# The product p @ W_ple moved from the attention stage to the opening, and x loaded a second time, turned, in a hybrid decoder layer

## The chip, the cores and the metric

The kernel runs on one core of one Trainium2 chip. The metric is the time of one execution on the device in microseconds (us). A core has five instruction streams that matter here: TensorE (PE, with its weight loads PEld), VectorE (DVE), ScalarE (ACT), GpSimd (POOL) and SyncE (SP), whose queue issues every DMA of this kernel, in order.

## The reference, cut to what matters

One decoder layer over 1024 tokens of width 1024, in float32:

```
h = RMSNorm(x)                                   # x: 1024 x 1024
proj = h @ W_in                                  # all projections, indexer keys i_k among them
o_A = gated DeltaNet(...) * SiLU(z_A)            # 4 heads
o_B = top-256 sparse attention(...) * SiLU(z_B)  # 8 heads
x = x + concat(o_A, o_B) @ W_out
gate = sigmoid(RMSNorm(x) @ W_gate + b_gate)
x = x + (p @ W_ple) * gate                       # p: 1024 x 256, W_ple: 256 x 1024
```

p @ W_ple depends on nothing else in the layer; it is needed only in the last line.

## The kernel before

Activations are held turned, features on the 128 partitions and tokens along the row, so that a projection is a chain of matmuls with a weight tile held in the array and 512 tokens streamed. For precision each float32 operand is split into a high part (ScalarE, a copy rounded to the matmul's type) and a low part (the rest, on VectorE or GpSimd), and `mm3` (line 778) takes three matmuls, hi·hi, hi·lo and lo·hi, for each product.

The program is recorded first and then ordered: the class `Plan` (from line 276) takes every instruction as an operation with a price (`price`, 339), list-schedules them (`forward` 466, `backward` 521), scores some orders by playing them (`play` 422) and issues the best (`issue` 556). Every instruction issued there has line 576 in the profile, so the rows are told apart by tile names. `keep_in_program_order` ties an operation to the one recorded before it on its engine.

The stages, in order:

- **The opening** (`start`, 795). `x_dma` (752) loads x in eight blocks of 128 tokens (tile `xt`, 512 KB each, five buffers), the norm's gain (`gcol`), `w_small` in two parts (`raws`; the columns for K, V and the small projections) and the weights of the indexer's keys (`raww`). `spread_gain` (807) turns the gain into a row tile by 8 transposes; 10 and 24 transposes of the identity around it keep TensorE running. For each block j: `front` (820) takes the sum of squares on ScalarE (`sq`), the reciprocal root on GpSimd (`rs`, two instructions) and x·r·gain on VectorE (`xn`); `turn` (831) makes 8 transposes on TensorE into two PSUM tiles (`xT`); `back` (841) copies them as `hThi` (ScalarE) and `hTlo` (VectorE); `small` (924) is 24 matmuls of 272 columns (`sm`) with the split `w_small` (`his`, `los`), evicted to `sm` and `kv` by ScalarE. Then `ik` (849): 48 matmuls of 512 columns in all, `Pik`.
- **Projections, indexer, DeltaNet** (60 to 540 us): a stream of weight jobs (class `Stream`) with chains of the other work woven in. Weights come as `raww`, split into `hiw` (ScalarE) and `low` (GpSimd).
- **Attention** (from 538 us): scores `S`, softmax on VectorE, ScalarE and GpSimd (`P`), transposes `pt`, products `pv`. The last z projections (`Pbz`) and then the jobs of the string `tail` in `jobs` (1560) fill TensorE beside it: "L" is a job of p @ W_ple, "M" loads the mixer's output, "A" to "D" are the output projection (`oA` to `oD`), "G" and "H" the gate (`g`).
- **p @ W_ple before**: `tail_open` (1842) calls `load_p` (1871), which loads p turned and splits it (`praw`, `pTh`, `pTl`). Eight jobs `ple_job` (1882), one for each quarter of W_ple and half of the tokens, make 12 matmuls of 512 columns each (`ple`), two evictions (`plt`) and two DMAs of 256 KB to memory (`pled`). The gate job (1963) loads them back (`pld`).

## Time and profile before

| | us |
|---|---|
| three runs | 863.83, 865.32, 2914.96 |
| their median | 865.32 |
| the profiled execution, its own time | 864.6 |
| its span, first to last instruction | 862.9 |
| TensorE busy in the span | 836.3 |

The run of 2914.96 us stands apart by a factor of three and is not used. The span is the part of the execution that the trace covers; the profiled execution's own time is 1.7 us more. A busy engine is one with an instruction in flight; TensorE's matmuls overlap, so a row's mean duration is longer than the distance from one matmul to the next.

### The profile page before, as it was taken

The numbers are of one execution on the slowest core, as the hardware profiler recorded it, in microseconds if no ns is written. First come the engines' busy times: TensorE is split into PE (matmuls) and PEld (weight loads), VectorE is DVE, ScalarE is ACT, GpSimd is POOL, SyncE is SP. The second block draws the span as 40 slices with busy tenths as digits, with TensorE's granted clock in tenths as the row PEclk, the third lists the DMA queues.
The fourth block names the chain that finished last, engine by engine and source line by source line (L and its number), as shares of the span: only waits on it lengthen the run. The fifth ranks groups of instructions, "written<-read, shape, count | busy, mean of one in ns | idle before, by whom it ended". The sixth has DMA issues, their size and how long they took to land.

```text
span 862.9 us, 15480 instructions
## 1 busy us (share of the span) xinstructions
PE 836.3 (97%) x5231; PEld 704.6 (82%) x5231; DVE 599.6 (69%) x1394; ACT 581.1 (67%) x1289; POOL 478.6 (55%) x651
## 2 busy tenths in 40 slices
PE   7999999999999999989999999899999999999996
PEld 6887888988778888878878888688888888787885
DVE  5535555567899878898887675978767687646344
ACT  5536465545868988889988843998876577655432
POOL 1162221312765766485775744588775587658841
PEclk9999999999999999999999999899999999999999
DMA  7123111132223222223123225885535321346453
GB/s 274 51 86 99 51 60 36 47 84 66 68 66 99 72 71 60 59 100 91 39 71 99 74 91 181 253 269 181 161 112 172 133 63 50 101 132 220 140 182 105
DMA packets 79455, 94.23 MB, mean 109 GB/s; under 512 B 24176, under 2 KB 40592, under 8 KB 79248
## 3 DMA queue, kind: packets, MB, share of 16 engines
q1 hardware_dynamic: 79376, 93.25, 34.2%
q8 instruction: 41, 0.67, 0.4%
q14 instruction: 38, 0.31, 0.1%
HBM read 67.77 MB, written 25.45 MB: 108 GB/s over the span
## 4 chain that ended last, share of the span: by engine, by line
PE 86%; DVE 4%; DMA 3%; ACT 3%; SPq 1%; issue 1%; POOL 1%; DVEq 0%; ACTq 0%; POOLq 0%
PE g L576 10%; PE Piq L576 8%; PE Pav L576 5%; PE Paz L576 5%; PE lg L576 5%; PE Paq L576 5%; PE Pbq L576 4%; PE Pbz L576 4%; PE pv L576 4%; PE S L576 4%; PE pt L576 4%; PE Pak L576 3%; PE ple L576 3%; PE sm L576 2%; PE po L576 1%; PE xT L576 1%
## 5 line engine op out<-in xcount | busy, mean ns | idle before, releaser
L576 POOL TENSOR_TENSOR low<-raww,hiw 128x512 fp32r<-128x512 f32 x138 | 186.8, 1355 | 170.7 <-ACT hiw L576 108.8
L576 ACT ACTIVATE hiw<-raww 128x512 fp32r<-128x512 f32 x138 | 86.4, 631 | 80.0 <-PE g L576 16.6
L576 ACT ACTIVATE junka<-score,nt 128x1024 bf16<-128x1024 int16 (+1 forms) x96 | 110.3, 1149 | 1.3
L576 DVE TENSOR_SCALAR_CACHE_REDUCE junk<-score,cand 128x384 bf16<-128x384 f32 (+2 forms) x96 | 70.8, 738 | 0.9
L576 POOL TENSOR_SCALAR P<-P,rsum 128x128 f32<-128x128 f32 (+7 forms) x64 | 50.2, 790 | 27.9 <-DVE rsum L576 21.4
L576 ACT ACTIVATE relu<-lg 128x384 f32<-128x384 f32 (+3 forms) x80 | 40.4, 526 | 34.7 <-PE lg L576 32.9
L576 ACT ACTIVATE P<-P,nm,rq 128x128 f32<-128x128 f32 (+7 forms) x64 | 55.2, 864 | 9.9 <-DVE nm L576 9.2
L576 POOL TENSOR_SCALAR nt<-acca,upa 128x1 f32<-128x1 f32 x96 | 34.9, 364 | 46.0 <-ACT junka L576 43.3
L576 DVE SCALAR_TENSOR_TENSOR score<-relu,sm,score 128x384 f32<-128x384 f32 (+5 forms) x42 | 45.7, 1097 | 20.6 <-ACT relu L576 20.1
L576 DVE TENSOR_TENSOR pl<-pt,ph 128x512 fp32r<-128x512 f32 x72 | 48.4, 687 | 13.9 <-ACT ph L576 12.4
L576 ACT ACTIVATE ph<-pt 128x512 fp32r<-128x512 f32 x72 | 42.0, 596 | 22.6 <-PE pt L576 21.8
L576 PE MATMUL S<-kst,qT 128*128 128x384 f32 (+4 forms) x192 | 55.0, 365 | 1.5 <-DVE mx L576 1.5
L576 PE MATMUL pt<-ident,P 128*128 128x128 f32 x288 | 51.7, 278 | 1.2 <-POOL P L576 0.6
L576 PEld LDWEIGHTS pt<-ident,P 128*128 128x128 f32 x288 | 38.1, 143 | 12.8 <-DVE pl L576 1.4
L576 PEld LDWEIGHTS S<-kst,qT 128*128 128x128 f32 x192 | 35.0, 195 | 8.2 <-DVE mx L576 2.5
L576 PE MATMUL Piq<-hThi,low 128*128 128x256 f32 (+1 forms) x128 | 40.7, 344 | 0.0
L576 PE MATMUL Piq<-hThi,hiw 128*128 128x256 f32 (+1 forms) x128 | 40.1, 343 | 0.0
L576 PE MATMUL Piq<-hTlo,hiw 128*128 128x256 f32 (+1 forms) x128 | 38.9, 339 | 0.0
L576 DVE TENSOR_TENSOR gth<-g,rb 128x512 f32<-128x512 f32 x16 | 11.1, 692 | 37.6 <-PE g L576 30.7
L576 DVE CUSTOM_DVE_ANT_0 P<-S,score 128x384 f32<-128x384 f32 (+3 forms) x48 | 28.6, 598 | 11.8 <-PE S L576 9.1
L576 PE MATMUL pv<-ph,vst 128*128 128x512 f32 x72 | 29.9, 416 | 0.0
L576 PE MATMUL pv<-pl,vst 128*128 128x512 f32 x72 | 29.8, 414 | 0.0
(623 smaller groups left out, 2825.6 us busy)
## 6 DMA issues: line engine op xcount, KB each, us to landing
raww<-in_w_ct_dram SPq DMA_DIRECT2D x66, 256.0 KB
raww<-in_w_out_dram SPq DMA_DIRECT2D x32, 256.0 KB
raww<-in_w_gate_dram SPq DMA_DIRECT2D x32, 256.0 KB
xt<-in_x_dram SPq DMA_DIRECT2D x8, 512.0 KB
pled<-plt SPq DMA_DIRECT2D x16, 256.0 KB
pld<-pled SPq DMA_DIRECT2D x16, 256.0 KB
out_dram<-gth SPq DMA_DIRECT2D x16, 256.0 KB
scr<-gcd SPq DMA_DIRECT2D x8, 256.0 KB
```

The costliest lines, as they stand in the source:

```text
L576: r = getattr(getattr(self.nc, o.eng), fn)(*[real(x) for x in args], **{k: real(v) for k, v in kw.items()})
```

## The change

- x is loaded a second time as `xc`, turned by the host's layout (`lay_out`), 512 KB a block in four buffers. The 64 transposes of x and the 8 of the gain go, and so do `xn` and `gain`. In their place `turn` makes one transpose that spreads r over the partitions (`rp`), and VectorE scales xc into PSUM: four instructions of 128 columns by gain and r, and one of 512 by r alone, for which GpSimd has multiplied the second half of xc by the gain.
- p @ W_ple becomes the opening's first work: its first chunk of p and two parts of W_ple lead SP's queue (p's first chunk in two halves), `ple_out(0, 0)` and `ple_out(1, 0)` come before x's first block, and six more stand one beside each of the blocks 1 to 6. p's chunks share the buffers of `xt`; `phi` and `plo` are p's parts. The evictions and the DMAs to `pled` come with them. The "L" jobs leave the tail.
- 30 transposes of the identity stand ahead in one piece (`warm`), and most ties to program order in the opening are dropped.
- The planner's prices change: a DMA occupies SP's queue for 400 and not 120, the backward pass counts a DMA's bytes, and an order's score is that of the play without jitter plus the mean of two with half the jitter.

```diff
-TL, TG = 3, 6
+TG, PLT = 6, 3
-WARM, WARM2 = 10, 24
+WARM = 30
-JITTER = (1, 2, 3)
-
-
+JITTER, UNEVEN = (1, 2), 524288
...
-            op.occ, op.bytes = 120, int(np.prod(o.ix.shape)) * SIZE[o.dt]
+            op.occ, op.bytes = 400, int(np.prod(o.ix.shape)) * SIZE[o.dt]
...
-                t = sum(self.play(o, seed) for seed in JITTER)
+                t = self.score(o)
                 if t < self.best:
                     self.best, order = t, o
         self.issue(order)
+
+    def score(self, order):
+        return self.play(order, 0) + sum(self.play(order, seed) for seed in JITTER) / len(JITTER)
...
-                occ *= 1 + (o.i * 40503 + seed * 30011) % 65536 / 262144
+                occ *= 1 + (o.i * 40503 + seed * 30011) % 65536 / UNEVEN
...
-            free[e] = s + o.occ
+            free[e] = s + max(o.occ, o.bytes / 280)
...
-        self.xt = [self.xpool.tile([128, D], F32, name="xt") for j in range(8)]
-        self.gain = self.xpool.tile([128, D], F32, name="gain", bufs=1)
-        load = lambda j: self.nc.sync.dma_start(self.xt[j], self.a["x"][j * 128:(j + 1) * 128, :])
+        self.xt, self.xc = [], []
+
+        keep = self.tc.keep_in_program_order
+
+        def load(j):
+            self.xt.append(self.xpool.tile([128, D], F32, name="xt"))
+            self.xc.append(self.xpool.tile([128, 8, 128], F32, name="xc", bufs=4))
+            keep(self.nc.sync.dma_start(self.xt[j], self.a["x"][j * 128:(j + 1) * 128, :]))
+            keep(self.nc.sync.dma_start(self.xc[j], self.a["xc"][j]))
...
+        self.gcol = self.xpool.tile([128, 8], F32, name="gcol", bufs=1)
+        self.praw, self.wpl = [], []
+
+        def load_p(n):
+            self.praw.append(self.xpool.tile([128, 2, 512], F32, name="praw", tag="xt"))
+            if n:
+                keep(self.nc.sync.dma_start(self.praw[n], self.a["pT"][n]))
+                return
+            keep(self.nc.sync.dma_start(self.praw[n][:, 0], self.a["pT"][n][:, 0]))
+            load_w(0)
+            keep(self.nc.sync.dma_start(self.praw[n][:, 1], self.a["pT"][n][:, 1]))
+
+        def load_w(e):
+            self.wpl.append(self.wp.tile([128, 4, 128], F32, name="raww", bufs=2))
+            keep(self.nc.sync.dma_start(self.wpl[e], self.a["w_ple"][e]))
+        load_p(0)
+        keep(self.nc.sync.dma_start(self.gcol, self.a["gains"][:, 16:24]))
+        load(0)
+        load_w(1)
+        for g in range(2):
+            keep(self.nc.sync.dma_start(self.wsm[g], self.a["w_small"][:, 4 * g:4 * g + 4]))
+        load(1)
+        load_p(1)
+        for j in range(2, 4):
+            load(j)
+        keep = lambda x: x
+        for e in range(2, 4):
+            load_w(e)
...
-            def spread_gain():
-                ps = [pp.tile([128, 4, 128], F32, name="xT") for _ in range(3)]
...
+            def warm(n):
+                ps = pp.tile([128, 4, 128], F32, name="xT", bufs=4)
+                for k in range(n):
+                    self.tc.keep_in_program_order(nc.tensor.transpose(ps[:, k % 4], self.ident, self.ident))
...
-                n = p.tile([128, D], F32, name="xn", bufs=2)
-                keep(nc.vector.scalar_tensor_tensor(n, x, r, self.gain, op0=OP.mult, op1=OP.mult))
-                return n
-
-            def turn(n):
-                out = []
-                for g in range(2):
-                    ps = pp.tile([128, 4, 128], F32, name="xT")
-                    for k in range(4):
-                        o = (4 * g + k) * 128
-                        keep(nc.tensor.transpose(ps[:, k], n[:, o:o + 128], self.ident))
-                    out.append(ps)
+                nc.gpsimd.tensor_tensor(xc[:, 4:8], xc[:, 4:8],
+                                        self.gcol[:, 4:8, None].to_broadcast([128, 4, 128]), op=OP.mult)
+                return r
+
+            def turn(j, r):
+                xc = self.xc[j]
+                rp = pp.tile([128, 128], F32, name="rp", bufs=1)
+                nc.tensor.transpose(rp, r.to_broadcast([128, 128]), self.ident)
+                out = [pp.tile([128, 4, 128], F32, name="xT", bufs=4) for g in range(2)]
+                for k in range(4):
+                    nc.vector.scalar_tensor_tensor(out[0][:, k], xc[:, k], self.gcol[:, k:k + 1], rp,
+                                                        op0=OP.mult, op1=OP.mult)
+                nc.vector.tensor_tensor(out[1], xc[:, 4:8], rp[:, None, :].to_broadcast([128, 4, 128]), op=OP.mult)
                 return out
...
+            def ple(e):
+                if e < 2:
+                    hi = self.plp.tile([128, 2, 512], F32R, name="phi", bufs=2)
+                    lo = self.plp.tile([128, 2, 512], F32R, name="plo", bufs=2)
+                    pt.append((hi, lo))
+                    if e:
+                        nc.scalar.activation(hi, self.praw[e], AF.Copy)
+                        nc.gpsimd.tensor_tensor(lo, self.praw[e], hi.bitcast(F32), op=OP.subtract)
+                    else:
+                        nc.scalar.activation(hi[:, 0], self.praw[e][:, 0], AF.Copy)
+                        nc.vector.tensor_tensor(lo[:, 0], self.praw[e][:, 0], hi[:, 0].bitcast(F32), op=OP.subtract)
+                whi = self.wp.tile([128, 4, 128], F32R, name="hiw", bufs=4)
+                wlo = self.wp.tile([128, 4, 128], F32R, name="low", bufs=4)
+                if e:
+                    nc.scalar.activation(whi, self.wpl[e], AF.Copy)
+                if not e:
+                    nc.scalar.activation(whi, self.wpl[e], AF.Copy)
+                    nc.scalar.activation(hi[:, 1], self.praw[e][:, 1], AF.Copy)
+                (nc.gpsimd if e else nc.vector).tensor_tensor(wlo, self.wpl[e], whi.bitcast(F32), op=OP.subtract)
+                wp.append((whi, wlo))
+                if not e:
+                    nc.vector.tensor_tensor(lo[:, 1], self.praw[e][:, 1], hi[:, 1].bitcast(F32), op=OP.subtract)
+
+            def ple_out(e, n):
+                (ph, pl), (whi, wlo) = pt[n], wp[e]
+                for j in range(2):
+                    ps = self.mm_ps(f"ple{e}_{n}")
+                    for k in range(2):
+                        self.mm3(ps, whi[:, 2 * j + k], wlo[:, 2 * j + k], ph[:, k], pl[:, k], k == 0, k == 1)
+                    t = self.plp.tile([128, 512], F32, name="plt", bufs=PLT)
+                    nc.scalar.activation(t, ps, AF.Copy, scale=0.5)
+                    nc.sync.dma_start(self.pled[n, 2 * e + j], t)
+
+            pt, wp = [], []
+            self.pled = self.tc.dram_tile([2, 8, 128, 512], F32, name="pled")
...
+            warm(WARM)
+            ple(0)
+            ple_out(0, 0)
+            ple(1)
+            ple_out(1, 0)
+            r = front(0)
+            ps, sm = turn(0, r), ()
+            later = {1: ((0, 1),), 2: ((1, 1),), 3: ((2, 0),), 4: ((2, 1),), 5: ((3, 0),), 6: ((3, 1),)}
             for j in range(9):
-                if j < 7:
-                    n = front(j + 1)
+                for e, n in later.get(j, ()):
+                    if e > 1 and n == 0:
+                        ple(e)
+                    ple_out(e, n)
+                if j == 0:
+                    self.small_split(0)
                 if j < 8:
                     back(j, ps)
+                if j < 7:
+                    r = front(j + 1)
                 if j == 0:
                     self.small_split(1)
                 for _ in sm:
                     pass
-                if j < 7:
-                    ps = turn(n)
                 if j < 8:
-                    if j == 6:
+                    if j == 5:
                         whi, wlo = self.split_w4("ik", self.wik)
                     sm = self.small(j)
                     next(sm)
+                if j < 7:
+                    ps = turn(j + 1, r)
+                if j == 7:
+                    ik(0)
             self.stream.prep(2)
-            ik(0)
             ik(1)
             self.k_norm()
         self.xpool_cm.__exit__(None, None, None)
+        self.plcm.close()
...
-        tail = "L" * TL + "M"
+        tail = "M"
         for d in range(8):
-            tail += "A" + "L" * ((8 - TL) * (d + 1) // 8 - (8 - TL) * d // 8)
+            tail += "A"
         tail += "M" + "C" * 8 + "B" * 8 + "G" * TG + "D" * 8 + "G" * (8 - TG) + "H" * 8
         for c in tail:
             i = cnt[c] = cnt.get(c, -1) + 1
-            if c == "L":
-                self.ple_job(st, i % 4, i // 4)
-            elif c == "M":
+            if c == "M":
...
-        self.pled = self.tc.dram_tile([2, 8, 128, 512], F32, name="pled")
-        self.load_p()
...
-    def ple_job(self, st, e, n):
-        nc = self.nc
-
-        def body(w):
-            (hi, lo), = w
-            ph, pl = self.pT[n]
...
+    o["xc"] = np.ascontiguousarray(g["x"][0].reshape(8, 128, 8, 128).transpose(0, 3, 2, 1))
...
-    o["pT"] = np.ascontiguousarray(g["p"][0, 0].T)
+    o["pT"] = np.ascontiguousarray(g["p"][0, 0].T.reshape(2, 128, 2, 512).transpose(2, 1, 0, 3))
```

TensorE's order at the start of the program, before (names: `sm_134` is the first small block):

```order
L576 MATMUL xT<-ident 128x128 x10
L576 MATMUL xT<-ident,gcol 128x128 x8
L576 MATMUL xT<-ident 128x128 x24
L576 MATMUL xT<-ident,xn 128x128 x16
L576 MATMUL sm_134<-his,hThi 128x272
L576 MATMUL sm_134<-los,hThi 128x272
L576 MATMUL sm_134<-his,hTlo 128x272
```

And with the change (`ple_0_126` and `ple_0_135` are the two halves of the first product):

```order
L581 MATMUL xT<-ident 128x128 x30
L581 MATMUL ple_0_126<-phi,hiw 128x512
L581 MATMUL ple_0_126<-plo,hiw 128x512
L581 MATMUL ple_0_135<-phi,hiw 128x512
L581 MATMUL ple_0_135<-plo,hiw 128x512
L581 MATMUL ple_0_126<-phi,low 128x512
L581 MATMUL ple_0_126<-phi,hiw 128x512
L581 MATMUL ple_0_135<-phi,low 128x512
L581 MATMUL ple_0_135<-phi,hiw 128x512
L581 MATMUL ple_0_126<-plo,hiw 128x512
```

The first product stands where the gain's transposes were. Behind the rows shown come the first `rp`, the 12 matmuls of the second product and then, with the last one among them, the first small block.

ScalarE's order at the start, before:

```order
L576 ACT_TABLE_LOAD
L576 ACTIVATE sq,ss<-xt 128x1024
L576 ACTIVATE his<-raws 128x1088
L576 ACTIVATE sq,ss<-xt 128x1024
L576 ACTIVATE hThi<-xT 128x4x128 x2
L576 ACTIVATE his<-raws 128x1088
L576 ACTIVATE sq,ss<-xt 128x1024
L576 ACTIVATE hThi<-xT 128x4x128 x2
L576 ACTIVATE sm<-sm_134 128x16
L576 ACTIVATE kv<-sm_134 128x256
```

And with the change, from its fifth instruction on (ahead stand the table load and the splits `phi`, `hiw`, `phi`; `ple_0_142` is the second product, `sm_275` the first small block):

```order
L581 ACTIVATE sq,ss<-xt 128x1024
L581 ACTIVATE plt<-ple_0_126 128x512
L581 ACTIVATE plt<-ple_0_135 128x512
L581 ACTIVATE hiw<-raww 128x512
L581 ACTIVATE his<-raws 128x1088
L581 ACTIVATE hThi<-xT 128x4x128 x2
L581 ACTIVATE his<-raws 128x1088
L581 ACTIVATE plt<-ple_0_142 128x512
L581 ACTIVATE sq,ss<-xt 128x1024
L581 ACTIVATE kv<-sm_275 128x256
L581 ACTIVATE sm<-sm_275 128x16
L581 ACTIVATE phi<-praw 128x1024
```

Two evictions and a split of W_ple now stand between the first `sq` and the two `his`, and p's second chunk, `phi` with 1024 columns, stands between the first small block's evictions and the next `hThi`.

TensorE's order at the attention's first blocks, before, where the first job of the tail begins:

```order
L576 MATMUL S_0_6699<-kst,qT 128x384 x2
L576 MATMUL S_1_6705<-kst,qT 128x384 x2
L576 MATMUL pv_1_6708<-ph,vst 128x512
L576 MATMUL pv_1_6708<-pl,vst 128x512
L576 MATMUL S_2_6726<-kst,qT 128x384 x2
L576 MATMUL pt_1_6732<-ident,P_4_6610 128x128
L576 MATMUL pt_1_6732<-ident,P_5_6618 128x128
L576 MATMUL pt_1_6740<-ident,P_4_6610 128x128
L576 MATMUL pt_1_6740<-ident,P_5_6618 128x128
L576 MATMUL S_3_6746<-kst,qT 128x384 x2
L576 MATMUL ple_0_6490<-pTh,hiw 128x512
```

And with the change, where the first job of the tail begins:

```order
L581 MATMUL pt_0_7003<-ident,P_2_6861 128x128
L581 MATMUL pt_0_7003<-ident,P_3_6872 128x128
L581 MATMUL pv_1_7022<-ph,vst 128x512
L581 MATMUL pv_1_7022<-pl,vst 128x512
L581 MATMUL pv_1_7022<-ph,vst 128x512
L581 MATMUL pv_1_7022<-pl,vst 128x512
L581 MATMUL S_0_7027<-kst,qT 128x512 x2
L581 MATMUL S_1_7032<-kst,qT 128x512 x2
L581 MATMUL S_2_7056<-kst,qT 128x512 x2
L581 MATMUL S_3_7069<-kst,qT 128x512 x2
L581 MATMUL oA__6869<-m0Ah,hiw 128x512
```

In both a stretch of `S`, `pt` and `pv` without other matmuls ends where the tail's first job starts, a product before and an `oA` now. It stood at scores of 384 columns, and now reaches those of 512. Behind the attention's first S stand 25 matmuls `Pbz` before and 57 now.

## Rows read from the trace of the kernel before

**Rows 1.** The page: its first line and the busy line of TensorE (busy us, share of the span, instructions).

```profile
span 862.9 us, 15480 instructions
PE 836.3 (97%) x5231; PEld 704.6 (82%) x5231; DVE 599.6 (69%) x1394; ACT 581.1 (67%) x1289; POOL 478.6 (55%) x651
```

**Rows 2.** The list of waits, TensorE alone, over the whole span: who waited, for whom, us in total, times, longest.

```profile
PE xT L576 <- DMA gcol<-in_gains_dram: 3.2, 1, 3.2
...
PE xT L576 <- DVE xn L576: 2.3, 2, 1.8
...
PE ple L576 <- ACT pTh L576: 1.0, 1, 1.0
```

**Rows 3.** Windows: the start up to the first transpose of x. The columns are the stretch, its length, then busy us and instructions of TensorE, its weight loads, VectorE, ScalarE and GpSimd, the granted clock of TensorE, the DMA share and GB/s.

```profile
0.00:13.39 13.39, 8.28 (x42) 7.88 (x43) 5.48 (x13) 4.69 (x6) 2.44 (x13) 1.00 0.78 289
```

**Rows 4.** The timeline of the opening, TensorE and ScalarE: start us, us, engine, line, operation, output and inputs, count, and in brackets the idle time before it and what ended it.

```profile
1.90 2.40 PE L576 MATMUL xT<-ident 128*128 128x128 f32 x10 [1.90 <-DVE ident L576]
...
4.68 1.06 ACT L576 ACTIVATE sq<-xt 128x1024 bf16<-128x1024 f32 x1 [2.61 <-DMA xt<-in_x_dram]
...
6.01 1.11 ACT L576 ACTIVATE his<-raws 128x1088 fp32r<-128x1088 f32 x1 [0.18 <-DMA raws<-in_w_small_dram]
...
7.38 1.06 ACT L576 ACTIVATE sq<-xt 128x1024 bf16<-128x1024 f32 x1 [0.25 <-DMA xt<-in_x_dram]
...
7.51 1.97 PE L576 MATMUL xT<-ident,gcol 128*128 128x128 f32 x8 [3.21 <-DMA gcol<-in_gains_dram]
...
9.27 4.29 PE L576 MATMUL xT<-ident 128*128 128x128 f32 x24
...
13.39 1.91 PE L576 MATMUL xT<-ident,xn 128*128 128x128 f32 x16
...
18.84 0.29 PE L576 MATMUL sm<-his,hTlo 128*128 128x272 f32 x1
```

**Rows 5.** Two windows of the opening, for the transfers: the stretch, its length, the granted clock, the DMA share and GB/s.

```profile
6.00:8.00 2.00, 1.00 1.04 411
22.00:26.00 4.00, 1.00 0.70 229
```

**Rows 6.** Groups by line and shape, 0 to 62 us: engine, operation, output and inputs, shapes, count, then busy us, mean ns of one, and the idle time before them. The last two rows are from the views of the tiles S and xT: their numbers are ns min/median/max and the first and last start in us.

```profile
L576 DVE TENSOR_TENSOR hTlo<-xT,hThi 128x512 fp32r<-128x512 f32 x16 | 10.3, 683 | 1.8 <-ACT hThi L576 1.8
...
L576 ACT ACTIVATE hThi<-xT 128x512 fp32r<-128x512 f32 x16 | 8.7, 601 | 6.5 <-PE xT L576 6.5
L576 ACT ACTIVATE sq<-xt 128x1024 bf16<-128x1024 f32 x8 | 8.5, 1059 | 2.9 <-DMA xt<-in_x_dram 2.9
...
L576 POOL TENSOR_TENSOR low<-raww,hiw 128x512 fp32r<-128x512 f32 x5 | 6.7, 1350 | 5.3 <-ACT hiw L576 5.3
...
L576 POOL TENSOR_TENSOR rs<-rs,mhalf 128x1 f32<-128x1 f32 x8 | 4.4, 553 | 0.7
L576 ACT ACTIVATE hiw<-raww 128x512 fp32r<-128x512 f32 x6 | 3.7, 633 | 1.9 <-DMA raww<-in_w_ct_dram 1.7
L576 ACT ACTIVATE kv<-sm 128x256 f32<-128x256 f32 x8 | 3.0, 379 | 0.0
...
L576 DVE TENSOR_TENSOR los<-raws,his 128x1088 fp32r<-128x1088 f32 x2 | 2.6, 1288 | 0.2 <-ACT his L576 0.2
...
L576 ACT ACTIVATE his<-raws 128x1088 fp32r<-128x1088 f32 x2 | 2.2, 1114 | 0.2 <-DMA raws<-in_w_small_dram 0.2
...
L576 DVE SCALAR_TENSOR_TENSOR S<-S,egl,rec0c x6: 333/344/349, 265.5 to 297.0; 128x128 f32<-128x128 f32 x6
...
L576 PE MATMUL xT<-ident,xn x64: 271/272/303, 13.4 to 42.1; 128*128 128x128 f32 x64
```

**Rows 7.** The chain of work that ended last, in order of time, 0 to 60 us and 500 to 600 us: start us, us, what.

```profile
30.45 3.03 PE sm L576 x24
33.48 0.87 PE xT L576 x8
...
37.39 1.06 PE xT L576 x8
...
53.51 2.09 PE Pik L576 x9
...
562.75 2.28 PE ple L576 x10
```

**Rows 8.** The tile ple, the sum of p @ W_ple, and its eviction to plt: ns min/median/max, first and last start in us.

```profile
L576 PE MATMUL ple<-pTh,hiw x32: 389/397/497, 559.9 to 633.1; 128*128 128x512 f32 x32
...
L576 ACT ACTIVATE plt<-ple x16: 579/598/609, 565.1 to 637.4; 128x512 f32<-128x512 f32 x16
```

**Rows 9.** Windows over the first half of the attention, columns as in rows 3.

```profile
540.00:560.00 20.00, 16.88 (x82) 13.40 (x80) 18.67 (x82) 18.36 (x51) 11.57 (x20) 0.83 0.83 247
560.00:640.00 80.00, 80.00 (x414) 66.27 (x414) 62.25 (x183) 68.82 (x143) 61.33 (x59) 1.00 0.60 191
640.00:660.00 20.00, 20.00 (x105) 16.93 (x104) 13.84 (x39) 14.40 (x28) 14.62 (x14) 1.00 0.46 148
```

**Rows 10.** Windows at the attention's first blocks, columns as in rows 3.

```profile
550.00:552.00 2.00, 1.38 (x7) 1.07 (x7) 1.94 (x10) 1.95 (x6) 1.75 (x3) 0.91 0.92 228
552.00:558.00 6.00, 5.33 (x20) 4.50 (x20) 5.65 (x23) 5.90 (x17) 4.46 (x6) 0.50 1.01 322
558.00:560.00 2.00, 0.99 (x6) 0.67 (x4) 1.58 (x8) 1.94 (x5) 0.95 (x3) 0.88 0.56 134
```

More of the change, by code (lines that the diff above doesn't have):

```diff
@@ L738, in setup @@
         self.ikp = self.spcm.enter_context(self.pool("ik", side="left"))
+        self.plcm = ExitStack()
+        self.plp = self.plcm.enter_context(self.pool("pl", side="left"))
         self.x_dma()
@@ L803, in start @@
         with self.pool("p0", bufs=4) as p, self.pool("p0s", bufs=4, space=PSUM) as pp:
-            keep = self.tc.keep_in_program_order
-            def spread_gain():
-                ps = [pp.tile([128, 4, 128], F32, name="xT") for _ in range(3)]
-                for k in range(WARM):
-                    keep(nc.tensor.transpose(ps[2][:, k % 4], self.ident, self.ident))
-                for k in range(8):
-                    keep(nc.tensor.transpose(ps[k // 4][:, k % 4],
-                                             self.gcol[:, k:k + 1].to_broadcast([128, 128]), self.ident))
-                for g in range(2):
-                    self.tc.keep_in_program_order(
-                        nc.vector.tensor_copy(self.gain[:, 512 * g:512 * g + 512], ps[g].rearrange("p a b -> p (a b)")))
-                for k in range(WARM2):
-                    keep(nc.tensor.transpose(ps[2][:, k % 4], self.ident, self.ident))
+            def warm(n):
+                ps = pp.tile([128, 4, 128], F32, name="xT", bufs=4)
+                for k in range(n):
+                    self.tc.keep_in_program_order(nc.tensor.transpose(ps[:, k % 4], self.ident, self.ident))
@@ L924, in small @@
     def small(self, j):
-        nc, keep = self.nc, self.tc.keep_in_program_order
+        nc = self.nc
         ps = self.mm_ps(f"sm_{j}", SMALL)
@@ L931, in small @@
                 hi, lo = self.hThi[:, 4 * g + k, s], self.hTlo[:, 4 * g + k, s]
-                keep(nc.tensor.matmul(ps, hi, whi[:, k], start=(g == 0 and k == 0), stop=False))
-                keep(nc.tensor.matmul(ps, hi, wlo[:, k], start=False, stop=False))
-                keep(nc.tensor.matmul(ps, lo, whi[:, k], start=False, stop=(g == 1 and k == 3)))
+                nc.tensor.matmul(ps, hi, whi[:, k], start=(g == 0 and k == 0), stop=False)
+                nc.tensor.matmul(ps, hi, wlo[:, k], start=False, stop=False)
+                nc.tensor.matmul(ps, lo, whi[:, k], start=False, stop=(g == 1 and k == 3))
             yield
-        keep(nc.scalar.activation(self.sm[:, j], ps[:, 256:272], AF.Copy))
-        keep(nc.scalar.activation(self.kv[:, j], ps[:, 0:256], AF.Copy))
+        nc.scalar.activation(self.sm[:, j], ps[:, 256:272], AF.Copy)
+        nc.scalar.activation(self.kv[:, j], ps[:, 0:256], AF.Copy)
     def params(self):
```

54 lines of the change are left out of this document (11 added, 43 removed).

## The prediction

> **What bounds the kernel now.** I read the page's busy line first: TensorE is busy for 836.3 of 862.9 us, so 26.6 us idle in all [rows 1]. The list of who made it wait has 3.2 and 2.3 us in the opening at its top, and after the opening a single wait of 1.0 us that this change touches, for p's split [rows 2]. So outside the opening nearly every instruction taken off TensorE is worth its issue time; inside it, what counts is when useful work starts and which wait ends last. Busy is not useful there: the 8.28 us of the first 13.39 us [rows 3] are all transposes of the identity and of the gain, and x's first transpose starts at 13.39 [rows 4].
>
> The change has two places to gain: those 13.4 us, into which the product can be put, and the transposes of x, which go. It has one to lose: the opening now waits for more splits on ScalarE and VectorE. I cut the time in three.
>
> **A: up to the end of the first small block.** Before, its last matmul starts at 18.84 and lasts 0.29: 19.1 [rows 4].
>
> After, data first. x's first 0.52 MB let ScalarE start at 4.68, w_small's 0.56 MB at 6.01, the next 0.52 MB of x at 7.38 [rows 4]: 0.4 MB per us, as the 411 GB/s of the window beside it [rows 5]. In the new order the first half of p's first chunk, W_ple's first part and the other half land by that rate at about 4.0, 4.7 and 5.3; x0, its turned copy, W_ple's second part and the two parts of w_small at 6.6, 7.9, 8.6, 10.0 and 11.4. Three splits of 0.63 us on ScalarE [rows 6] are through by 6.0, their low parts on VectorE (0.68 each, the row of hTlo) by 6.8.
>
> TensorE has 30 dummy transposes ahead of it from 1.90. The gain's eight take from 7.51 to 9.27, 0.22 each; the 24 behind them until 13.39, 0.17 each [rows 4]. Thirty take 5.1 to 6.6 us, so the first product starts between 7.0 and 8.5; I take 7.5. Its 12 matmuls cost 0.228 each (ten in 2.28, [rows 7]): done at 10.2.
>
> Then ScalarE's order decides: two evictions (0.60 each, [rows 8]), W_ple's second split 0.63, the first his 1.11, two hThi 1.1, the second his 1.11 [rows 6]. From 10.2 these end at 11.4, 12.0, 13.1, 14.2 and 15.3. The second product can start at 12.0 (a wait of 1.8), needs GpSimd's low part at 13.4 (1.35) and ends about 15.2. The small block's first half runs on to 16.7; its second half wants the second los (15.3 + 1.29 = 16.6) and then the last hTlo (17.3), and ends near 18.6. The turned x is not late for this: sq from 6.6 to 7.7, then the accumulator's read and GpSimd's two instructions, about 1 us (the longer one 0.55), one transpose behind the first product at 10.3, four scaled copies of at most 0.34 (the nearest row, the same operation with a PSUM operand) and one pass of 0.68 [rows 6]: 12.4.
>
> A gains 0.5 us, with 24 of the 96 product matmuls done in it. If TensorE is still at half pace when the product starts, its 24 matmuls cost up to 24 x 0.228 = 5.5 us more, part of it inside the 1.8 us wait: 4 us is the far end. With the waits half as long it is 2 us better, the near end.
>
> **B: from there until the Pik matmuls are done.** Before: seven blocks at 3.03, six groups of transposes at 0.87 to 1.06 (0.97 taken), 48 Pik at 0.23 [rows 7], and 2.3 us of waiting for xn [rows 2]: 21.2 + 5.8 + 11.0 + 2.3 = 40.3, ending at 59.4. After: the same 21.2 and 11.0, 72 product matmuls 16.4, and seven transposes of r. A single transpose between matmuls has no row; it costs between 0.11 (an eighth of 0.87, [rows 7]) and 0.27 (one's own duration, [rows 6]), or 0.8 to 1.9; I take 0.9, since they stand between running matmuls. One new wait: behind the small block ScalarE has kv (0.38), a shorter copy and then p's second chunk at sq's 1.06, the same width, before the third product can start: 18.6 to 20.2, or 1.6 us, and 0.6 us more for hThi and hTlo. Later blocks have a product of 2.7 us beside 3.03 of the small block, about 5.9 us a block, against some 4.6 on ScalarE (sq, two hThi, two evictions, kv, a share of the splits), 3.4 on VectorE (1.4 + 0.7 + 1.3) and 2.5 on GpSimd; I charge nothing there, and 0.5 us a block, 3 in all, if that cover fails. B is 21.2 + 11.0 + 16.4 + 0.9 + 2.2 = 51.7, ending at 70.3. The opening ends 10.9 us later than before.
>
> The transfers hide beside it. The opening now moves x twice (8.4 MB), p and W_ple (2.1), w_small and ik's weights (1.6) and the 16 writes of pled (4.2): 16.3 MB, which at 411 GB/s end at about 43 us. SP's queue is in order, so a write that waits for an eviction holds the loads behind it; the first such write stands ahead of x2 and is released near 11, while what was issued before it lands until 15.
>
> **C: the rest.** 96 product matmuls leave 560 to 638 us [rows 8]: 96 x 0.228 = 21.9 us, in a stretch in which TensorE is busy for 80.00 of 80 us [rows 9]. With them goes the 1.0 us wait for p's split. ScalarE loses 16 evictions, 8 splits of W_ple and 4 of p there, 17 us, and GpSimd 12 splits, 16 us, so neither takes TensorE's place. VectorE keeps its work, 62.25 us in those 80, which now shares 78 us with what follows (13.84 of the 20 behind, [rows 9]): 76 of 78 would be tight, but the attention goes on beside the output projections, and what slips finds TensorE work there.
>
> At the attention's first blocks both orders have a stretch without fill, and I cost that edit at nothing. The lost work there is now about 5.2 us: busy time by granted clock adds to 1.38 x 0.91 + 5.33 x 0.50 + 0.99 x 0.88 = 4.8 of 10 us [rows 10]. It could vanish (-5), as 57 Pbz matmuls instead of 25, 7.3 us more, now stand behind the first S, or grow by 4, as the unfilled piece now reaches wider scores.
>
> The planner's prices change too, so everything is reordered. With little idle time outside the opening I cost that at nothing, and 4 us to either side.
>
> **Sum.** +10.9 - 21.9 - 1.0 = -12.0 on the profiled execution's 864.6 us: 852.6, say 852.5. Its time lies in the middle of the two runs, 863.83 and 865.32, so nothing is corrected. That is 1.4%, under the 2% (17.3 us: 847.3 and 881.9) that a measurement of this kernel can tell from no change.
>
> **Rivals.**
> 1. The covers work better: A two us earlier, the 2.2 us of waits in B gone and half of the 5.2 us at the attention's entry recovered: 852.5 - 6.8 = 845.7, faster by over 2%. For it: fewer ScalarE instructions at that entry, where ScalarE is busy for 18.36 of 20 us [rows 9]. Against it: in the opening his and phi now stand in one queue. Chance 0.18.
> 2. The attention does not give the product's time back. If VectorE sets its pace, the 21.9 us become waits: all of it 864.6 + 10.9 = 875.5, half of it 864. For it: VectorE's 18.67 of 20 at the entry and 62.25 of 80 behind. Against it: 13.84 of 20 from 640 on. Chance 0.12.
> 3. The transfers bind the opening. At the 229 GB/s of a stretch with writes among its loads [rows 5], 16.3 MB end at 75 us and not 43, past B's 70.3: 5 us more, 857, and with the queue held by evictions perhaps 862. Against it: the last x is wanted only near 55. Chance 0.06.
> 4. Slower by over 2%: the fill is missed and the clock falls. [...] If the whole 21.9 us turn into such waits, spread over 560 to 620, three stretches of 20 us lose 3.4 us each as 540 to 560 does now (0.83 granted, [rows 9]), on top of 875.5: 886. It decides from the point at which more than 17 of the 21.9 us come back as waits. Chance 0.04.
> [...]
>
> **How the numbers follow.** Forecast 0.60. Its own ends are 2 + 2.2 + 3 us better (845) and 4 + 3 + 4 worse (863). The range 843 to 863 takes in rival 1, half of rival 2 and rival 3, and leaves out less than 2 in 10. Faster by over 2%: rival 1 and a small corner of the forecast, 0.22. Slower by over 2%: rival 4 and a corner of 2, 0.05. Within 2%: 0.73.
>
> **What would show it.** In the new profile: the first product matmul at 7 to 8.5 us, a wait of about 1.8 us for W_ple's second split at 10, the end of the first small block near 18.6, a wait for phi right behind it, the last Pik near 70; no product between 555 and 640; 72 transposes fewer on TensorE. The prediction is wrong if the first small block ends after 22 us, if the last Pik comes after 75, or if VectorE or ScalarE hold up TensorE for more than 10 us between 545 and 700.

## The result and the profile after

| | us |
|---|---|
| before, median (the three that agree of four) | 865.32 (863.83 to 867.52) |
| after, median of four runs | 855.97 (855.36 to 856.67) |
| after to before | 0.9889, 95% interval 0.9861 to 0.9918 |
| the profiled execution of after: its own time, its span | 856.67, 854.4 |

By the ratio 9.6 us of 865, 1.1%: within 2%, as forecast, and 3.5 us above the predicted 852.5. The run of before that stands apart (2914.96) is left out again, as is one such run each of e10 (1164.26) and e12 (4650.96).

The page of after answers [rows 1]: TensorE is busy for 6.9 us less, and idle for 25.0 us in place of 26.6.

```profile
span 854.4 us, 15369 instructions
PE 829.4 (97%) x5163; PEld 690.4 (81%) x5163; DVE 611.3 (72%) x1427; ACT 578.5 (68%) x1284; POOL 484.5 (57%) x651
```

The timeline of TensorE in the new opening, in answer to [rows 4]; in brackets, the idle time before an instruction and what ended it:

```profile
7.19 0.47 PE L581 MATMUL ple<-phi,hiw 128*128 128x512 f32 x1
...
9.83 0.40 PE L581 MATMUL ple<-phi,low 128*128 128x512 f32 x1
...
11.45 0.50 PE L581 MATMUL ple<-phi,hiw 128*128 128x512 f32 x1 [1.11 <-ACT hiw L581]
...
12.82 0.50 PE L581 MATMUL ple<-phi,low 128*128 128x512 f32 x1 [0.18 <-POOL low L581]
...
14.56 0.29 PE L581 MATMUL sm<-his,hThi 128*128 128x272 f32 x1
...
17.72 0.37 PE L581 MATMUL sm<-his,hTlo 128*128 128x272 f32 x1
19.58 0.50 PE L581 MATMUL ple<-phi,hiw 128*128 128x512 f32 x1 [1.49 <-ACT phi L581]
...
71.86 0.39 PE L581 MATMUL Pik<-hThi,low 128*128 128x512 f32 x1
```

The reader is to see the forecast sequence in its places: the product from 7.19, the wait for W_ple's second split, the first small block done at 18.09, the wait for phi, and the last Pik at 72.25. The first scores of the attention are the next mark; before, first, then after:

```profile
61.55 0.39 PE L576 MATMUL Pik<-hThi,low 128*128 128x512 f32 x1
...
538.24 0.40 PE L576 MATMUL S<-kst,qT 128*128 128x256 f32 x2
```

```profile
545.71 0.40 PE L581 MATMUL S<-kst,qT 128*128 128x256 f32 x2
```

With these marks the span falls into stages. Windows of before, then of after, columns as in [rows 3]:

```profile
0.00:60.00 60.00, 52.16 (x350) 48.71 (x351) 29.42 (x47) 29.24 (x63) 17.41 (x39) 1.00 0.41 139
60.00:538.20 478.20, 470.07 (x3346) 398.64 (x3345) 357.70 (x815) 340.97 (x821) 247.76 (x426) 1.00 0.25 76
538.20:640.00 101.80, 98.68 (x504) 81.22 (x503) 81.81 (x269) 88.67 (x196) 73.23 (x78) 0.97 0.65 206
640.00:862.90 222.90, 215.35 (x1037) 176.03 (x1035) 130.63 (x263) 122.20 (x211) 140.20 (x110) 0.99 0.40 128
```

```profile
0.00:72.00 72.00, 66.97 (x380) 58.61 (x381) 36.65 (x80) 42.09 (x87) 30.32 (x50) 1.00 0.76 262
72.00:545.70 473.70, 464.78 (x3312) 389.62 (x3311) 358.22 (x815) 340.54 (x820) 253.50 (x426) 1.00 0.25 76
545.70:640.00 94.30, 90.98 (x475) 72.63 (x474) 82.11 (x273) 78.69 (x176) 65.54 (x72) 1.00 0.53 165
640.00:854.40 214.40, 206.72 (x1000) 169.51 (x999) 134.34 (x260) 117.16 (x204) 135.13 (x105) 1.00 0.39 126
```

The stages must be compared at equal work, since the planner moves fill across the marks. Six Pak matmuls now start before the last Pik, eleven before; 57 Pbz stand behind the first S, 25 before. At 0.228 us each [rows 7], before's marks moved to after's division of the work are 60.8 and 530.9.

| stage, at equal work | before | after | difference |
|---|---|---|---|
| opening, to the last Pik | 60.8 | 72.25 | +11.5 |
| middle, to the first S | 470.1 | 473.5 | +3.3 |
| attention, to the end | 332.0 | 308.7 | -23.3 |

The sum is -8.5, the change of the span (the differences are rounded from more digits). The middle stood in the forecast's sum with 0.

In the attention the hole is where it was forecast to be, at the first blocks without fill, but at a granted clock of 1.00. In answer to [rows 9]:

```profile
560.00:580.00 20.00, 17.57 (x84) 12.69 (x83) 18.64 (x64) 19.24 (x47) 11.81 (x16) 1.00 0.48 160
580.00:600.00 20.00, 19.69 (x103) 15.30 (x101) 17.27 (x50) 19.41 (x42) 18.93 (x19) 1.00 0.78 239
```

### The profile page after: what moved, and what is told of

The parts are those of the page before. It is cut to its first block, busy times and chain, and to the rows that moved or that the text cites. A ratio compares the mean times of both kernels' runs of the same rounds, so it can differ in the third digit from the quotient of the medians.

```text
span 854.4 us, 15369 instructions
## 1 busy us (share of the span) xinstructions
PE 829.4 (97%) x5163; PEld 690.4 (81%) x5163; DVE 611.3 (72%) x1427; ACT 578.5 (68%) x1284; POOL 484.5 (57%) x651
## 4 chain that ended last, share of the span: by engine, by line
PE 72%; DVE 9%; ACT 6%; DMA 5%; POOL 4%; issue 3%; SPq 1%; ACTq 0%; DVEq 0%; POOLq 0%
PE g L581 7%; PE Piq L581 7%; PE lg L581 5%; PE Pbz L581 4%; PE Pak L581 4%; PE Pbq L581 4%; PE Paq L581 4%; PE S L581 3%; PE pt L581 3%; PE Pav L581 3%; PE pv L581 3%; PE Paz L581 3%; PE sm L581 3%; PE ple L581 2%; POOL low L581 2%
## 5 line engine op out<-in xcount | busy, mean ns | idle before, releaser
L581 POOL TENSOR_TENSOR low<-raww,hiw 128x512 fp32r<-128x512 f32 x133 | 180.0, 1358 | 164.7 <-ACT hiw L581 124.8
L581 ACT ACTIVATE hiw<-raww 128x512 fp32r<-128x512 f32 x134 | 84.0, 630 | 69.7 <-PE g L581 21.9
L581 POOL TENSOR_SCALAR nt<-acca,upa 128x1 f32<-128x1 f32 x96 | 39.5, 412 | 43.9 <-ACT junka L581 42.1
L581 PE MATMUL S<-kst,qT 128*128 128x384 f32 (+4 forms) x192 | 59.0, 361 | 0.7 <-DVE qT L581 0.4
L581 DVE SCALAR_TENSOR_TENSOR score<-relu,sm,score 128x384 f32<-128x384 f32 (+5 forms) x42 | 42.3, 1020 | 23.2 <-ACT relu L581 23.0
L581 PEld LDWEIGHTS pt<-ident,P 128*128 128x128 f32 x288 | 37.3, 140 | 12.9 <-DVE pl L581 2.3
```

The lines of the kernel that those rows point to most:

```text
L581: r = getattr(getattr(self.nc, o.eng), fn)(*[real(x) for x in args], **{k: real(v) for k, v in kw.items()})
```

## The experiments

All times are medians; a ratio is to runs of the kernel before on the same chip. The theory: TensorE sets the pace nearly everywhere, so the attention gives back the product's issue time, and the opening pays the same time less what it had idle. The rivals: VectorE keeps the attention's time, the transfers bind the opening, the planner's new prices are what helps or hurts, and the turned x alone is the gain.

**e3_before_no_product: does the attention give the time back?**

```diff
-        tail = "L" * TL + "M"
+        tail = "M"
-        self.load_p()
-                nc.sync.dma_start(pp, self.pled[n, e])
+                nc.sync.dma_start(pp, a["xT"][e * 128:e * 128 + 128, n * 512:n * 512 + 512])
```

The kernel before with p @ W_ple left out altogether.

> The kernel before without p @ W_ple: neither p's split nor the 96 product matmuls, their evictions and writes are there, and the gate job loads a piece of x in their place. It shows what the attention gives back when the product leaves, with nothing added to the opening and the old planner. If TensorE sets the attention's pace: 864.6 - 21.9 - 1.0 = 841.7, so 838 to 845. If VectorE or ScalarE set it (the second rival of the prediction): 850 to 864.

Measured: 843.12 us beside 865.48, ratio 0.9736 (0.9693 to 0.9780): 22.4 us, against 22.9 in the sum. TensorE's windows without the product show no hole that swallows it:

```profile
540.00:560.00 20.00, 19.84 (x108) 16.09 (x107) 18.78 (x69) 19.65 (x50) 11.10 (x16) 1.00 0.36 114
560.00:640.00 80.00, 76.19 (x392) 61.86 (x392) 67.73 (x194) 61.28 (x123) 60.05 (x56) 1.00 0.49 153
```

Rival 2 of the prediction falls: 3.8 us idle from 560 to 640, not 11 or 22. At equal work its attention is 23.8 us shorter than that of before. The changed kernel is 12.9 us longer than this one (855.97 - 843.12), but it has the turned x too. With x turned by TensorE as here (e4 below) the product in the opening makes 17.6 us (860.71 - 843.12), still most of the 22.4 that it costs in the attention.

**e1_old_planner and e2_before_new_planner: the prices.** The changed kernel with the old prices, and the kernel before with the new ones (the two directions of this edit):

```diff
-            op.occ, op.bytes = 120, int(np.prod(o.ix.shape)) * SIZE[o.dt]
+            op.occ, op.bytes = 400, int(np.prod(o.ix.shape)) * SIZE[o.dt]
-                t = sum(self.play(o, seed) for seed in JITTER)
+                t = self.play(o, 0) + sum(self.play(o, seed) for seed in JITTER) / len(JITTER)
-JITTER = (1, 2, 3)
+JITTER = (1, 2)
-            free[e] = s + o.occ
+            free[e] = s + max(o.occ, o.bytes / 280)
```

(and half the jitter)

> The changed kernel with the planner's old prices (a DMA at 120, three jittered plays, no bytes in the backward pass). The work is the same. Between the opening and the attention the changed kernel lost 3.3 us that the prediction did not have. Theory A, the new prices cost it: this kernel gains them back, 852 to 854. Theory B, any reordering moves a few us either way and the prices mean nothing: anywhere from 852 to 861, with the opening's end (last Pik, less the Pak matmuls mixed in) within 2 us of 70.9. Theory C, the new prices are part of the gain: 859 or more.

> The kernel before with the planner's new prices and nothing else. Theory A (the new prices cost 3 us): 867 to 869. Theory B (reordering without direction): 861 to 870, whatever its sign here not that of the other kernel. Theory C (the prices give part of the gain): 858 to 862.

Measured: 856.95 (0.9898, 0.9857 to 0.9939) and 864.5 (0.9981, 0.9960 to 1.0001). Neither direction is told from nothing. Both fall in theory B's ranges; A and C, as they were put, fall. (Without its Pak e1's opening ends at 72.9, at the edge of B's 2 us.) But the equal totals hide large pieces. In e2 TensorE stands for 8.84 us ahead of its first S, for p's split, where before has 1.0:

```profile
548.44 1.65 PE L576 MATMUL ple<-pTh,hiw 128*128 128x512 f32 x3 [8.84 <-ACT pTh L576]
```

The granted clock is 0.68 from 540 to 550 and 0.81 from 550 to 560 there. e1 has a clock of 0.62 from 447 to 456 and of 0.83 from 20 to 30.

**e10_other_seeds: other seeds, the same order.**

```diff
-JITTER, UNEVEN = (1, 2), 524288
+JITTER, UNEVEN = (3, 4), 524288
```

> The same work as in the changed kernel, with two other seeds for the planner's jitter, so that another order wins. If an order that the planner picks is worth no more than a draw, the time is 853 to 859 and the time between the last Pik and the first attention scores moves by some 3 us at equal work. If the order of the changed kernel is a lucky one, it is 859 or more.

Measured: 855.55, ratio 0.9880 (0.9835 to 0.9925). The planner chose the order of the changed kernel again: on all five engines every instruction stands where it stands there, by name and shape (5163 on TensorE alone). So neither value of the expectation is tested; this is the changed kernel run once more, and it shows how far one order varies. Its middle stage at equal work is 472.3 us here, 472.4 and 472.6 in e11 and e12, 473.5 in the profile after.

With other orders the middle, worked out in the same way, is 472.1 (e9) to 474.8 (e7) where the clock in it is 1.00. It is 474.9 in e3, whose edit touches the attention alone (a mean clock of 0.994 over its whole span), and some 477 in e1 and e2, with the clocks of 0.62 and 0.68 given above. The 470.1 of before is the shortest of all, although its clock is 0.72 from 451 to 457. So an order alone moves this stage by a few us, and about 1 us of the +3.3 is what one order varies by; that an order of the changed kernel must lose it is not shown.

**e4_product_only and e5_turned_x_only: one part at a time.** In e4 x is turned by TensorE, as before; in e5 xc is loaded and the product stays in the attention.

```diff
# e4, from the changed kernel
-            keep(self.nc.sync.dma_start(self.xc[j], self.a["xc"][j]))
+                n = p.tile([128, D], F32, name="xn", bufs=2)
+                nc.vector.scalar_tensor_tensor(n, x, r, self.gain, op0=OP.mult, op1=OP.mult)
+                        nc.tensor.transpose(ps[:, k], n[:, o:o + 128], self.ident)
# e5, from the changed kernel
-            ple_out(0, 0)
-            ple_out(1, 0)
-        tail = "M"
+        tail = "L" * TL + "M"
```

> The changed kernel without the turned load: x is turned by 8 transposes a block on TensorE from xn, and the gain is spread by 8 transposes behind the first product; p @ W_ple stays the opening's first work. If TensorE bounds the opening, 72 transposes come back and 8 go: 7.5 + 0.9 - 0.9 = 7.5 us later than the changed kernel, 863 to 865, the opening's end near 78. Rival, the transposes fit into waits (for phi, for hiw): 857 to 859.

> The kernel before with the turned load alone: p @ W_ple stays in the attention, the planner has its new prices, 30 dummy transposes lead. If TensorE bounds the opening, it saves 7.5 - 0.9 = 6.6 us of transposes and the 2.3 us of waits for xn, and starts its first small block no later than before: 856 to 859, about as much as the whole change. Rival, the first block now waits for the turned x on VectorE and nothing is saved ahead of it: 861 to 864.

Measured: e4 860.71, ratio 0.9939 (0.9915 to 0.9963), the last Pik at 75.6; e5 862.73, ratio 0.9977 (0.9954 to 0.9999). By the ratios that is -5.3 and -2.0 us, beside -9.6 for both; the 2.3 us by which the whole exceeds their sum is within the intervals. e4 came out better than expected, between its two values: the opening ends 3.4 us after that of the changed kernel, not 7.5, and TensorE is idle in it for 2.6 us in place of 5.0, so that some of the transposes stand in what were waits.

e5's opening ends at 57.2 (the last Pik, at equal work), 3.6 us before that of the kernel before, where 8.9 were expected. Its waits from 0 to 90 us (the first two of the list), VectorE around the longest, and its second ten us:

```profile
PE sm L581 <- DVE los L581: 4.1, 2, 3.2
PE sm L581 <- ACT hThi L581: 2.3, 1, 2.3
```

```profile
14.89 1.52 DVE L581 SCALAR_TENSOR_TENSOR xT<-xc,gcol,rp 128x128 f32<-128x128 f32 x4
16.32 1.28 DVE L581 TENSOR_TENSOR los<-raws,his 128x1088 fp32r<-128x1088 f32 x1
```

```profile
10.00:20.00 10.00, 5.58 (x24) 4.86 (x25) 6.95 (x12) 5.98 (x11) 4.79 (x9) 0.64 1.02 408
```

Without the transposes TensorE reaches the first small block at 10.13 in place of 15.06, and then stands. The rival's case shows: the second los, for which it waits longest, stands on VectorE behind the scaling of block 1's turned x, though its his was done at 13.1. The DMA engines are full (share 1.02), but this wait is not for a transfer. The granted clock is 0.64 here and 0.85 in the next ten us, in which TensorE is busy throughout; busy time by the clock that is missing (5.58 x 0.36 + 10.00 x 0.15) is 3.5 us, an estimate.

e5 then waits for p's split at the attention's start, as e2 does, which has the new prices too:

```profile
PE ple L581 <- ACT pTh L581: 8.4, 1, 8.4
```

So e5 is to be set beside e2: 1.8 us less in the medians, and an opening that ends 2.9 us sooner (57.2 and 60.1). Beside the product the turned x shortens the opening by 3.4 (e4 and the changed kernel). It is worth about 3 us there either way; that the two parts help each other is not shown.

**e6_xc_twice and e9_late_loads: more bytes, two misses.**

```diff
             keep(self.nc.sync.dma_start(self.xc[j], self.a["xc"][j]))
+            keep(self.nc.sync.dma_start(self.xc[j], self.a["xc"][j]))                 # e6, every j
+            for _ in range(2 if j > 3 else 0):                                        # e9
+                self.nc.sync.dma_start(self.xc[j], self.a["xc"][j])
```

> The changed kernel with every turned block loaded twice into the same buffer, 4.2 MB more in the opening, 20.5 in all. If the transfers hide beside TensorE: within 3 us of the changed kernel's 856, the first small block at most 3 us later since the second copy lands ahead of w_small. If they bind the opening: 4.2 MB at 410 GB/s, 10 us more, 866.

> The turned x of blocks 4 to 7 is loaded three times instead of once, so the opening moves the same 4.2 MB more as when every block was loaded twice (13 us slower), but none of them stands ahead of the first small block. If those 13 us came from the head of the queue (the splits of W_ple and w_small late, TensorE idle, its granted clock at 0.66 to 0.84 from 10 to 40 us), the time stays within 3 us of 856 and the granted clock at 1.00. If the volume as such binds the opening, the time is 864 or more again, with TensorE waiting for blocks 4 to 7.

Measured: 869.47 (1.0047, 1.0027 to 1.0067) and 869.97 (1.0065, 1.0041 to 1.0088). This looks like rival 3 of the prediction, transfers that bind, and for e9 my theory of the queue's head was refuted as I had put it: no extra load stands ahead of its first small block, and it is slow all the same. But the planner sees these loads. In e6 the second load of a block, into the same tile, waited in SP's queue for the first one's landing, and the planner had it ahead of a part of W_ple and of w_small:

```profile
5.51 0.57 SPq L581 DMA_DIRECT2D xt<-in_x_dram  x1
10.16 0.33 SPq L581 DMA_DIRECT2D xc<-in_xc_dram  x1
10.59 0.38 SPq L581 DMA_DIRECT2D raww<-in_w_ple_dram  x1
11.02 0.90 SPq L581 DMA_DIRECT2D raws<-in_w_small_dram  x2
```

In the changed kernel w_small is issued at 4.08. In e9 the queue is that of the changed kernel up to 12 us, but ScalarE's order is another; e9's ScalarE, and then that of the changed kernel:

```profile
10.29 1.08 ACT L581 ACTIVATE plt<-ple 128x512 f32<-128x512 f32 x2 [4.58 <-PE ple L581]
11.26 1.06 ACT L581 ACTIVATE sq<-xt 128x1024 bf16<-128x1024 f32 x1
12.21 0.20 ACT L581 ACTIVATION_READ_ACCUMULATOR sq<-xt 128x1 f32 x1
12.30 0.63 ACT L581 ACTIVATE hiw<-raww 128x512 fp32r<-128x512 f32 x1
```

```profile
7.63 1.06 ACT L581 ACTIVATE sq<-xt 128x1024 bf16<-128x1024 f32 x1 [2.02 <-DMA xt<-in_x_dram]
8.60 0.19 ACT L581 ACTIVATION_READ_ACCUMULATOR sq<-xt 128x1 f32 x1
9.80 1.08 ACT L581 ACTIVATE plt<-ple 128x512 f32<-128x512 f32 x2 [1.01 <-PE ple L581]
10.77 0.63 ACT L581 ACTIVATE hiw<-raww 128x512 fp32r<-128x512 f32 x1
```

sq, which filled idle time of ScalarE, now stands behind the evictions, W_ple's split stands behind it, and the first small block starts at 18.90 and not 14.56. That is 4.3 of the 13.8 us by which e9's last Pik comes later; more is lost further on, as at blocks 5 and 7, where TensorE waits 2.25 us each time for the turned x. And in both runs a load waits in SP's queue for the one before it into the same tile: 21.0 us in all in e6, 18.6 in e9. Neither run separates the transfers from the order and from these waits.

**e11_late_copies and e12_early_copies: more bytes at a fixed order.** The copies go in where the finished order is issued, so the planner does not see them; all other rows of the order stay.

```diff
+            if o.eng == "sync" and isinstance(o.args[0], View) and not o.args[0].t.dram and o.args[0].t.kw["name"] == "xc":
+                c, xcs = xcs, xcs + 1
+                for k in range(2 if c > 3 else 0):            # e11; c < 4 in e12
+                    d = self.tc.dram_tile([128, 8, 128], F32, name=f"xs{c}{k}")
+                    self.tc.keep_in_program_order(self.nc.sync.dma_start(d, real(o.args[1])))
```

> The changed kernel with eight copies of 0.5 MB from memory to memory put into SP's queue, two behind the load of each of the turned blocks 4 to 7, after the planner has fixed its order: every engine's order stays that of the changed kernel, and the copies wait for nothing. 4.2 MB more between some 20 and 45 us. If the two earlier kernels with double loads were slow because the planner saw the loads and put other instructions first in the opening, and the transfers themselves are hidden there, the time is 855 to 859. If the volume binds, it is 863 or more, with TensorE waiting for blocks 4 to 7.

> The same eight copies, two behind the load of each of the turned blocks 0 to 3, so that two stand ahead of W_ple's second part and w_small and four ahead of p's second chunk. If the head of the queue is what has no slack, these land 2.6 and 5.2 us later (1.05 MB at 0.41 MB per us each), the first small block starts 3 to 5 us later, and the time is 859 to 864, more if the granted clock falls. If the head has slack too, it is within 3 us of 856.

Measured: e11 857.8, ratio 0.9920 (0.9893 to 0.9946), its profiled span 854.3, that of the changed kernel 854.4; e12 860.36, ratio 0.9949 (0.9929 to 0.9969), span 859.6. Both as the theory has it: 4.2 MB more cost the late stretch some 2 us (the last Pik at 74.0, 1.8 us later), though the DMA engines are full there:

```profile
30.00:40.00 10.00, 9.67 (x60) 8.46 (x59) 6.12 (x13) 6.02 (x16) 4.50 (x6) 1.00 1.04 384
40.00:50.00 10.00, 10.00 (x65) 9.13 (x64) 6.13 (x13) 5.08 (x12) 4.77 (x7) 1.00 1.00 401
50.00:72.00 22.00, 21.27 (x113) 17.49 (x112) 6.19 (x12) 8.65 (x21) 7.86 (x10) 1.00 0.69 235
```

Up to 50 us TensorE is on time with the changed kernel; the 1.8 us come behind that, where, for one, an eviction on ScalarE waits 3.20 us for a store of pled. e11 differs from e9 in two things, the order and copies that wait for no tile; which of them makes e9's 13 us is not separated, but the bytes alone do not.

At the head the copies cost 4 to 5 us. e12's TensorE, ScalarE's split for which it waits, and the window:

```profile
10.28 0.32 PE L581 MATMUL rp<-ident,rs 128*128 128x128 f32 x1 [0.64 <-POOL rs L581]
13.18 0.79 PE L581 MATMUL ple<-phi,hiw 128*128 128x512 f32 x1 [2.58 <-ACT hiw L581]
13.77 0.63 PE L581 MATMUL ple<-plo,hiw 128*128 128x512 f32 x1
14.20 0.63 PE L581 MATMUL ple<-phi,hiw 128*128 128x512 f32 x1
...
18.04 0.43 PE L581 MATMUL sm<-his,hThi 128*128 128x272 f32 x1
```

```profile
12.50 0.63 ACT L581 ACTIVATE hiw<-raww 128x512 fp32r<-128x512 f32 x1 [2.21 <-DMA raww<-in_w_ple_dram]
```

```profile
10.00:20.00 10.00, 7.14 (x25) 5.79 (x26) 5.81 (x9) 5.63 (x9) 3.70 (x6) 0.66 0.98 400
```

The wait for W_ple's second split is 1.5 us longer, and behind it the matmuls come 0.43 apart and not 0.23: the window 10 to 20 has a granted clock of 0.66 here, 1.00 in the changed kernel. The last Pik is at 77.6.

**e8_no_stores: fewer bytes.**

```diff
-                    nc.sync.dma_start(self.pled[n, 2 * e + j], t)
-                nc.sync.dma_start(pp, self.pled[n, e])
+                nc.sync.dma_start(pp, a["xT"][e * 128:e * 128 + 128, n * 512:n * 512 + 512])
```

> The sixteen stores of the product are left out (4.2 MB less in the opening; the gate reads other data of the same size, so the output is not the reference's). If the transfers are hidden behind TensorE's work from 20 us on, as the waits of the changed kernel say (0.2 us between 20 and 72), the time is 854 to 858, which is the spread of reordered plans. If the stores, which wait for evictions in SP's queue, hold up loads that TensorE needs, the time falls to 853 or less and the opening ends 3 us or more sooner than 72.3.

Measured: 856.21, ratio 0.9889 (0.9853 to 0.9924), the last Pik at 72.1. The planner sees this edit too, so the order is another here as well; within the spread of orders the stores cost nothing, though SP's queue stands long for them; its row in the changed kernel's list of waits, 0 to 110 us:

```profile
SPq L581 <- ACT plt L581: 28.1, 8, 4.4
```

**e7_phi_first: the wait for phi.**

```diff
+        if j == 0:
+            self.tc.edge(self.phi1, a, 0)
+            self.tc.edge(self.phi1, b, 0)
```

(phi1 is p's second chunk on ScalarE; a and b are the first block's two evictions)

> The changed kernel with one edge more for the planner: the split of p's second chunk stands before the evictions of the first small block on ScalarE, which was idle for 2.2 us there. The wait of 1.5 us for phi goes. If the opening is a chain of TensorE's work and its waits, the opening ends 1 to 1.5 us earlier, 854 to 855.5 unless the reordering behind moves more. If p's second chunk had not landed, the wait stays: 856 to 857.

Measured: 858.77, ratio 0.9919 (0.9890 to 0.9949), above both values. The wait went and another came in its place; TensorE, then ScalarE:

```profile
21.42 0.50 PE L581 MATMUL ple<-phi,hiw 128*128 128x512 f32 x1 [2.38 <-ACT plt L581]
```

```profile
17.25 1.06 ACT L581 ACTIVATE phi<-praw 128x1024 fp32r<-128x1024 f32 x1 [0.49 <-DMA praw<-in_pT_dram]
20.29 0.60 ACT L581 ACTIVATE hThi<-xT 128x512 fp32r<-128x512 f32 x1 [1.97 <-DVE xT L581]
20.78 0.59 ACT L581 ACTIVATE plt<-ple 128x512 f32<-128x512 f32 x1
```

phi is through at 18.3 (19.5 in the changed kernel), but the eviction that frees the product's PSUM tile stands behind a hThi that waits 1.97 us for VectorE. The opening ends 1.1 us later, the span 1.6.

## Why the prediction was right, and where it was off

- **A** (19.1 to 18.6): right, 18.09. The half pace of its far end did not show: the granted clock is 1.00 from 0 to 20, and the first product's matmuls come 0.23 us apart. The wait was 1.11 and not 1.8: the product began 0.3 sooner, and two evictions in a row took 1.08 us together, not 1.20, so that W_ple's second split was done at 11.4 and not 12.0.
- **B** (70.3): right, within 0.6. With the six Pak taken out the last Pik is at 70.9, and B is 52.8 long against 51.7. The wait for phi was 1.49 (1.6 forecast); the waits came out no longer than charged, and the rest counts as busy.
- **"The transfers hide beside it":** right behind the first block but for some 2 us, by e11, but too wide as it stood. At the head they don't hide (e12), and what was charged there, waits of 1.8 and 1.6 us, was the right kind of term.
- **C** (-21.9 - 1.0): right. The attention is 23.3 us shorter at equal work, and 23.8 in e3, whose time falls by 22.4 with nothing added to the opening.
- **Entry to the attention at 0:** within its bounds. The clock's 3 us there are regained (0.97 granted over 101.8 us before, 1.00 after), and 2.6 of them are lost again: TensorE's idle time from the first S on is 11.0 us, where 10.7 less p's 1.0 was to be left, and the other half stands in no wait.
- **Reordering at 0, 4 to either side:** the step that was mis-sized. It came out at +3.3 and makes nearly the whole difference between -12.0 and the span's -8.5. Only 0.8 us of it is idle time (8.92 against 8.13); the rest counts as busy, and it is not the clock, which is 1.00 in the middle after. Its size lies in the bound that was given, but "little idle time outside the opening" was the wrong reason for 0: an order can be longer without showing more waits, and by its profile before had a short one. Why the new order is longer stays open.

Rivals 2 and 4 did not come: 3.3 us idle and a granted clock of 1.00 from 545.7 to 640. Nor did rival 3: 4.2 MB more cost 1.8 us of the opening (e11). The falling clock of rival 4 did show in other runs, in stretches with waits: in the opening of e1, e5, e6, e9 and e12 (0.64 to 0.83 granted over ten us), and at the attention's entry in e2 (0.68 from 540 to 550) and e5 (0.57 from 538 to 550), around the wait for p's split. What lowers it is not shown. The 886 of rival 4 was my estimate from the 0.83 that before has from 540 to 560; in the changed kernel's attention, where the fill was taken out, no row shows a fall. Rival 1 had one of its parts, the clock at the entry, and lost it again.

## What to carry to other kernels

Independent work gains where the core waits for its first data, if its own operands head the queue and the loads that lead the path stay right behind it (eight copies put among them cost 4 to 5 us in e12); here the moved product, without the turned x, still cost 17.6 of its 22.4 us. Price a move stage by stage at equal work, with a term of a few us for the new order that a planner finds, since that moves stages which the change does not touch (the middle, +3.3 here). Look for stretches at a low granted clock before two orders are compared: equal totals can hide them (0.62 from 447 to 456 in e1, whose time is within 1.0 us of the changed kernel's). Add a suspected load behind the planner, not in front of it, or the experiment measures another order; and see that an edit of the planner's inputs has changed the order at all, for other seeds did not.

## What was not expected of the hardware

- Copies from memory to memory held the DMA engines at shares of 1.00 to 1.04 and 384 to 401 GB/s beside a TensorE that was busy for 19.67 of 20 us: its time over that stretch was not longer than without them (9.66 and 10.00 busy in the same two windows of the changed kernel). It lost behind it: busy for 21.27 of the 22 us from 50 to 72, where the changed kernel has 22.00.
- The granted clock was low around quite short waits; why is not shown. In e12 TensorE was idle for 0.64 us, made one transpose, and was idle for 2.58 more; the matmuls of the product behind that came 0.43 us apart, where those of the product ahead came 0.23 apart, and the clock is 0.66 from 10 to 20. In e1, around waits of 1.31 and 0.94 us with one matmul between, the clock is 0.50 from 22 to 24. In the changed kernel, with waits of 1.11 and 1.49 us, 8 us apart, it is 1.00 from 10 to 20 and from 20 to 30.
